# Modulation vectors accumulated on VectorE in two FFNs, convolution taps spread over the last layer, and the convolution's norm placed inside the pooling branch

## Chip, core and metric

The kernel runs on one core of a Trainium2 chip. The metric is device time of one execution in microseconds (us); the kernel before takes 2716.47 us (median of 3 runs).

## The reference, cut to what matters

Two transformer blocks of two layers each run one after the other, on 256 latent tokens and 256 context tokens, 1024 wide. Every layer is steered by six modulation vectors, made from a condition `c` (for the latent tokens) and `c_ctx` (for the context tokens); the last layer of a block needs the context's only for its first two vectors.

```python
# block 1, layer l
m_lat = split(silu(c) @ ada_w[l] + ada_b[l], 6)      # ada_w[l]: 1024 x 6144
m_ctx = split(silu(c_ctx) @ ada_w[l] + ada_b[l], 6)
h = x * (1 + m[1]) + m[0]
x = layer_norm(ALPHA * x + m[2] * mixer(h))
x = layer_norm(ALPHA * x + m[5] * conv_ffn(x * (1 + m[4]) + m[3]))
# block 2, layer l: the same six vectors from w_mod[l], b_mod[l], and
def token_mixer(h, hc, ...):
    u = h @ w_glu; u = u[:, :512] * sigmoid(u[:, 512:])
    u = depthwise_conv(u, conv_w, conv_b)             # 31 taps along the tokens, 512 channels
    y_a = silu(layer_norm(u)) @ w_conv_out
    y_b = differential_attention(h, hc) @ w_attn_out
    y_c = multiscale_pool(h @ w_p) @ w_pool_out
    g = sigmoid(h @ w_g + b_gate)
    return (g0 * y_a + g1 * y_b + g2 * y_c) @ w_out
swiglu(h) = (silu(h @ w1) * (h @ w2)) @ w_ffn_out
```

In the first layer of a block all 512 tokens are carried through, in the second only the 256 latent ones leave the mixer. All data are fp32.

## The kernel before

**Weights and products.** Each weight comes from memory as a 128x1024 tile `wr` (512 KB, `wload`, L143, issued on SP's queue, four buffers). `wsplit` (L149) makes from it a rounded high part `wh` on ScalarE (L154) and the rest `wl` on VectorE or GpSimd (L156), three buffers each. A product is then three matmuls: high by high, high by low, low by high (L163). One weight tile is 24 matmuls.

**Stages in time.** Block 1 layer 0 (mixer, then a 512-token FFN from about 340 us), block 1 layer 1 (mixer, then a 256-token FFN), block 2 layer 0 (mixer from 1110 us, 512-token FFN from about 1720), block 2 layer 1 (mixer from 2120 us, 256-token FFN from 2520). The attentions run under an order written out by `weave`: a list of main entries (one weight tile's products and the evictions that follow), between which the steps of the attention units are put. An entry that does one thing alone is marked `light`. Outside the attentions a scheduler orders the instructions of each engine by its own estimate of time; each engine then executes in that fixed order.

**Modulation vectors.** `ada` (L171) makes a list of work items for the vectors ("parts") of one layer: per part eight slices of 128 rows, then the bias, then a transposition. For a slice the raw tile is loaded and four TensorE matmuls (L195) multiply it by the conditions `cs`, each for 256 of the 1024 columns and each at its own group of 32 columns of the array; the eight slices of a part sum up in one PSUM bank. `run_ada` takes items off the list at fixed places, `stream_ada` puts them into the list of an attention. Block 1 layer 1 has its items begun in the first attention and the remaining 38 in the 512-token FFN that follows. The 58 items of block 2 layer 1 are spread over block 2 layer 0: two with each of its eight heads, the rest in the 512-token FFN.

**512-token FFN** (`ffn`, L1106). Up products come in pairs `j` (a gate tile and a value tile): pairs 0 to 3 for one half of the tokens and then for the other, pairs 4 to 10 for all 512, then the first half of the down products, pairs 11 to 21, and the second half. The products `gH`, `gL` of a pair have 14 buffers. Items of `ada` are taken one after each of the pairs 0 to 3 of the second half, two after each of the pairs 4 to 10, one after each down weight, one after each later pair, and what is left ahead of `mid`.

**Convolution and branches of block 2.** The 31 taps for four groups of 128 channels are 124 VectorE operations (`conv_taps`, L1601; L1605 and L1608), taken one by one from a generator. `tick` in `b2_attn` takes `rate` of them per light entry of the attention; `b2_branches` takes 15 after each of the eight output blocks of the attention's branch ("merged blocks", L1681), and the rest after it. Then `b2_conv_ln` normalises the convolution's result, and the pooling branch (`branch(2, ...)`) and the convolution's branch (`branch(0, ...)`) follow, each with eight merged blocks (L1684).

## Time and profile before

| | before |
|---|---|
| median of 3 runs | 2716.47 us (2715.8 to 2717.38) |
| profiled execution | 2717.76 us, its span 2716.0 us |
| TensorE (PE) busy | 2572.2 us, 95% |
| VectorE (DVE) busy | 1744.9 us, 64% |
| ScalarE (ACT) busy | 1230.1 us, 45% |
| GpSimd (POOL) busy | 405.1 us, 15% |
| mean granted clock of TensorE | 0.981 |
| HBM read | 408.59 MB |

The span runs from the first instruction to the last; the execution's own time holds 1.8 us more around it. Busy shares are averages over stages with different limits, so the windows below are read stage by stage. Matmuls overlap on TensorE: what one costs the queue is seen from the starts of its neighbours, not from its own length.

### The profile page before, as it was taken

Reading aid. Unit: us, or ns where it says so; the run is one execution under the profiler, and the core shown is the slowest. Engines: PE = TensorE matmul, PEld = TensorE weight load, DVE = VectorE, ACT = ScalarE, POOL = GpSimd, SP = SyncE. Lnnn points to the kernel's source line nnn. Section 1 sums busy time; section 2 is a strip of 40 time slices with the busy share of each in tenths; the row PEclk is TensorE's granted clock in tenths of the full one; section 3 lists DMA queues with packets and bytes.
Section 4 is the critical chain, followed back from the end, with each engine's and each line's share of the span. In section 5 each row is a group of like instructions: output and inputs, shape, how many; then the busy total and the mean of one; then the engine's idle time right before and its main releaser. Section 6 shows DMA issues by size and latency. Waiting matters only on the chain. (4 is left out here: it accounts for less than half of the span.)

```text
span 2716.0 us, 41732 instructions
## 1 busy us (share of the span) xinstructions
PE 2572.2 (95%) x16052; PEld 2196.6 (81%) x16052; DVE 1744.9 (64%) x3131; ACT 1230.1 (45%) x2327; POOL 405.1 (15%) x481
## 2 busy tenths in 40 slices
PE   7999899999998899999988999999999999789998
PEld 5787697778876798998976787877777999788997
DVE  5766785355887877577789546632236766986554
ACT  3554453134455555556652324522224566344443
POOL 4221100000121100444320000000000243100000
PEclk9999999999999999999999999999999999899999
DMA  8355765543556665532212234655445421246555
GB/s 274 100 160 173 252 212 174 164 128 118 179 174 230 206 228 182 170 112 90 90 62 78 79 101 156 196 170 162 146 125 161 146 81 65 88 150 197 168 183 148
DMA packets 129831, 412.43 MB, mean 152 GB/s; under 512 B 16640, under 2 KB 24992, under 8 KB 129632
## 3 DMA queue, kind: packets, MB, share of 16 engines
q1 hardware_dynamic: 119296, 386.45, 44.8%
q0 software_dynamic: 10048, 23.30, 2.8%
q8 instruction: 126, 2.06, 0.3%
q14 instruction: 73, 0.60, 0.1%
q10 hardware_dynamic: 288, 0.02, 0.0%
HBM read 408.59 MB, written 1.11 MB: 151 GB/s over the span
## 5 line engine op out<-in xcount | busy, mean ns | idle before, releaser
L154 ACT CAST wh<-wr 128x1024 fp32r<-128x1024 f32 (+2 forms) x580 | 572.3, 990 | 920.3 <-PE mm L163 653.1
L156 DVE TENSOR_TENSOR wl<-wr,wh 128x1024 fp32r<-128x1024 f32 (+2 forms) x494 | 571.3, 1159 | 452.3 <-ACT wh L154 448.9
L163 PE MATMUL mm<-hH,wh 128*128 128x256 f32 (+1 forms) x2176 | 714.1, 329 | 5.1 <-DVE sil L1144 2.3
L163 PE MATMUL mm<-hH,wl 128*128 128x256 f32 (+1 forms) x2176 | 707.9, 326 | 9.1 <-DVE wl L156 9.1
L163 PE MATMUL mm<-hL,wh 128*128 128x256 f32 (+1 forms) x2176 | 707.1, 325 | 0.0
L163 PEld LDWEIGHTS mm<-hH,wh 128*128 128x128 f32 x2176 | 419.0, 193 | 57.4 <-issue 18.3
L163 PEld LDWEIGHTS mm<-hH,wl 128*128 128x128 f32 x2176 | 419.1, 193 | 45.2 <-DVE wl L156 13.0
L163 PEld LDWEIGHTS mm<-hL,wh 128*128 128x128 f32 x2176 | 419.3, 193 | 30.7
L163 PE MATMUL mm<-wh,hH 128*128 128x384 f32 (+1 forms) x864 | 278.5, 322 | 0.7 <-DVE hH L308 0.7
L163 PE MATMUL mm<-wl,hH 128*128 128x384 f32 (+1 forms) x864 | 269.6, 312 | 2.8 <-DVE wl L156 1.8
L163 PE MATMUL mm<-wh,hL 128*128 128x384 f32 (+1 forms) x864 | 269.2, 312 | 0.3 <-DVE hL L312 0.3
L156 POOL TENSOR_TENSOR wl<-wr,wh 128x768 fp32r<-128x768 f32 (+1 forms) x86 | 182.5, 2126 | 260.4 <-ACT wh L154 183.6
L163 PE MATMUL mm<-wl,gH 128*128 128x512 f32 x528 | 205.9, 390 | 2.6 <-DVE wl L156 2.6
L163 PE MATMUL mm<-wh,gH 128*128 128x512 f32 x528 | 208.0, 395 | 0.0
L163 PE MATMUL mm<-wh,gL 128*128 128x512 f32 x528 | 205.9, 390 | 0.0
L163 PEld LDWEIGHTS mm<-wh,hH 128*128 128x128 f32 x864 | 163.9, 190 | 13.9 <-issue 11.0
L163 PEld LDWEIGHTS mm<-wl,hH 128*128 128x128 f32 x864 | 164.0, 190 | 6.2 <-DVE wl L156 2.7
L163 PEld LDWEIGHTS mm<-wh,hL 128*128 128x128 f32 x864 | 163.8, 190 | 0.5 <-DVE hL L312 0.5
L1608 DVE SCALAR_TENSOR_TENSOR cv<-u,cconv_w,cv 128x512 f32<-128x512 f32 (+1 forms) x240 | 162.1, 682 | 2.2
L262 POOL TENSOR_TENSOR rs_r<-rs_v,mhalf 128x1 f32<-128x1 f32 x44 | 40.0, 911 | 630.1 <-DVE rs_v L283 373.9
L163 PEld LDWEIGHTS mm<-wh,gH 128*128 128x128 f32 x528 | 99.1, 188 | 28.4 <-issue 8.6
L163 PEld LDWEIGHTS mm<-wl,gH 128*128 128x128 f32 x528 | 99.2, 188 | 23.3 <-DVE wl L156 3.5
(332 smaller groups left out, 3961.5 us busy)
## 6 DMA issues: line engine op xcount, KB each, us to landing
wr<-in_up SPq DMA_DIRECT2D x192, 512.0 KB, 4.3
wr<-in_dn SPq DMA_DIRECT2D x100, 512.0 KB, 3.7
wr<-in_w_mod SPq DMA_DIRECT2D x96, 512.0 KB, 4.3
wr<-in_ada_w SPq DMA_DIRECT2D x80, 512.0 KB, 4.2
wr<-in_wg SPq DMA_DIRECT2D x48, 512.0 KB, 3.6
wr<-in_glu SPq DMA_DIRECT2D x24, 512.0 KB, 4.2
wr<-in_qkv SPq DMA_DIRECT2D x32, 384.0 KB, 3.2
wr<-in_wo SPq DMA_DIRECT2D x24, 512.0 KB, 4.1
```

The costliest lines, as they stand in the source:

```text
L154: nc.scalar.copy(h[:, :n], w[:, :n])
L156: eng.tensor_tensor(l[:, :n], w[:, :n], h[:, :n], ALU.subtract)
L163: self.nc.tensor.matmul(o, s, m, start=start, stop=stop, skip_group_check=True)
L262: self.nc.gpsimd.tensor_tensor(o, i, self.mhalf[:, 0:n], ALU.pow)
L1608: nc.vector.scalar_tensor_tensor(o, u[:, :, j:j + 256], w[:, c, j:j + 1], o, ALU.mult, ALU.add)
```

## The change

Three things are changed.

1. While a 512-token FFN runs (from pair 4 up to `mid`), a slice of a modulation vector is not multiplied on TensorE. VectorE multiplies the raw tile by the condition's value of each partition and adds it to an accumulator of 128x1024 (`onto`): one accumulator per condition, one buffer each. At a part's last slice TensorE sums the accumulator over the partitions with four matmuls per condition against a vector of ones (`pick`). Parts whose context vector nobody reads (`ctx=2`: all but the first two of the second layers) have one accumulator, the others two. A part that was begun on TensorE goes on in the accumulator and is added to its bank. In block 2 layer 0 no items ride with the attention any more; all 58 go to the FFN, two after each later pair and three after pairs 20 and 21. No item is taken in pairs 0 to 3. `gH` and `gL` have 12 buffers.
2. In block 2's last layer every main entry ticks, not the light ones alone, at a rate of 0.6 instead of 1.5. The taps that are left after the attention are strewn, in both layers, evenly over the eight blocks of the attention's branch and the first five of the pooling branch.
3. The convolution's norm is issued after the fifth block of the pooling branch, not ahead of that branch.

```diff
@@ setup
+        self.pick = cp.tile([P, 33], F32, name="pick")
+        nc.gpsimd.memset(self.pick, 0.0)
+        nc.gpsimd.memset(self.pick[:, 1:2], 1.0)
@@ ada
-    def ada(self, key, blk, w, b, parts=(1, 0, 2, 4, 3, 5)):
+    def ada(self, key, blk, w, b, parts=(1, 0, 2, 4, 3, 5), ctx=6):
+            def quarter(st, j, a, x, start, stop):
+                nc.tensor.matmul(st["pa"][32 * j:32 * j + 32, 0:256], a, x[:, j * 256:(j + 1) * 256], start=start, stop=stop,
+                                 skip_group_check=True, tile_position=(0, 32 * j))
+
+            def onto(wt, st, k, rows):
+                if "acc" not in st:
+                    st["acc"] = [self.acc_pool.tile([P, D], F32, tag=f"acc{r}", name=self.nm("adacc"), bufs=1) for r in range(rows)]
+                    for r in range(rows):
+                        nc.vector.tensor_scalar(st["acc"][r], wt, cs[:, k, r:r + 1], None, ALU.mult)
+                else:
+                    for r in range(rows):
+                        nc.vector.scalar_tensor_tensor(st["acc"][r], wt, cs[:, k, r:r + 1], st["acc"][r], ALU.mult, ALU.add)
-            def prod(wt, m=m, k=0, st=st):
+            def prod(wt, m=m, k=0, st=st, rows=2 if parts.index(m) < ctx else 1):
...
-                for j in range(4):
-                    nc.tensor.matmul(st["pa"][32 * j:32 * j + 32, 0:256], cs[:, k, :], wt[:, j * 256:(j + 1) * 256],
-                                     start=(k == 0), stop=(k == 7), skip_group_check=True, tile_position=(0, 32 * j))
+                if self.acc_pool is not None:
+                    onto(wt, st, k, rows)
+                else:
+                    if "pa" not in st:
+                        st["pa"] = self.psum(self.ada_bank)
+                    for j in range(4):
+                        quarter(st, j, cs[:, k, :], wt, k == 0, k == 7 and "acc" not in st)
+                if k == 7 and "acc" in st:
+                    first = "pa" not in st
+                    if first:
+                        st["pa"] = self.psum(self.ada_bank)
+                    for r, a in enumerate(st["acc"]):
+                        for j in range(4):
+                            quarter(st, j, self.pick[:, 1 - r:33 - r], a, first and r == 0, r == len(st["acc"]) - 1)
@@ ffn
-                    nbuf = 14 if T == 512 else 22
+                    nbuf = 22 if T == 256 else 12
@@
                 for s in range(2):
                     for j in range(self.SKEW):
                         up_pair(j, s, s + 1)
-                        if s:
-                            self.run_ada(ada, 1)
+                self.acc_pool = pool
...
                 for j in range(11, 22):
                     up_pair(j, 0, 2)
-                    self.run_ada(ada, 1)
+                    self.run_ada(ada, 2 if j < 20 else 3)
                 self.run_ada(ada, 100)
+                self.acc_pool = None
@@ b2_attn
-            gr["extra"] = self.stream_ada(ws, ada, 2)
@@
-            if i > n and getattr(main[i], "light", True):
+            if i > n and (not full or getattr(main[i], "light", True)):
                 due[0] += rate
                 while due[0] >= 1:
                     due[0] -= 1
-                    next(taps, None)
+                    next(taps, lambda: None)()
@@ b2_branches
-                for _ in range(15):
-                    next(taps, None)
+                strew()
+
+            left = list(taps)
+            n = -(-len(left) // 13)
+
+            def strew():
+                for f in left[:n]:
+                    f()
+                del left[:n]
             branch(1, "wyb", 8, at, hook)
-            for _ in taps:
-                pass
             pools.close()
@@
-        self.b2_conv_ln(cp, cp, cb["pool"], l, T, nseg, cb["cv"], cc)
-        branch(2, "wyc", 4, mix, lambda oc: None)
+
+        def hook2(oc):
+            strew()
+            if oc == 4:
+                assert not left
+                self.b2_conv_ln(cp, cp, cb["pool"], l, T, nseg, cb["cv"], cc)
+        branch(2, "wyc", 4, mix, hook2)
@@ build
-            a0 += self.ada("b1l1", 1, A["ada_w"][1], A["ada_b"][1])
+            a0 += self.ada("b1l1", 1, A["ada_w"][1], A["ada_b"][1], ctx=2)
...
-            a3 = self.ada("b2l1", 2, A["w_mod"][1], A["b_mod"][1])
+            a3 = self.ada("b2l1", 2, A["w_mod"][1], A["b_mod"][1], ctx=2)
...
-            self.b2_mixer(1, 256, cb[1], lambda: after(1), ws, self.glu_items(ws, 1, cb[1], 0, 1), 1.5)
+            self.b2_mixer(1, 256, cb[1], lambda: after(1), ws, self.glu_items(ws, 1, cb[1], 0, 1), 0.6)
```

The taps' generator now yields functions, called where a tap was taken before. What the order of instructions makes of this is shown at three places; the line numbers are each kernel's own.

VectorE in the first 512-token FFN, one pair's work among the pairs 4 to 10. Before (`acc` are convolutions, `sil` and `gL` the pair's product, `wl` the next weights' low parts):

```order
L156 TENSOR_TENSOR wl_4891<-wr_4888,wh_4890 128x1024
L1121 SCALAR_TENSOR_TENSOR acc_4831<-mm_4772,conv_w_791_3357,acc_4831 128x2x255
L1122 SCALAR_TENSOR_TENSOR acc_4831<-mm_4772,conv_w_791_3357,acc_4831 128x2x255
L1121 SCALAR_TENSOR_TENSOR acc_4835<-mm_4803,conv_w_791_3357,acc_4835 128x2x255
L1122 SCALAR_TENSOR_TENSOR acc_4835<-mm_4803,conv_w_791_3357,acc_4835 128x2x255
L1141 TENSOR_TENSOR sil_4830<-sil_4830,acc_4831 128x512
L1150 TENSOR_TENSOR gL_4842<-sil_4830,gH_4841 128x512
L156 TENSOR_TENSOR wl_4951<-wr_4948,wh_4950 128x1024
L156 TENSOR_TENSOR wl_4982<-wr_4979,wh_4981 128x1024
```

Now (`adacc` is the accumulator):

```order
L1151 SCALAR_TENSOR_TENSOR acc_4622<-mm_4565,conv_w_791_3360,acc_4622 128x2x255
L204 SCALAR_TENSOR_TENSOR adacc_4552<-wr_4806,cs_85,adacc_4552 128x1024
L1152 SCALAR_TENSOR_TENSOR acc_4622<-mm_4565,conv_w_791_3360,acc_4622 128x2x255
L204 SCALAR_TENSOR_TENSOR adacc_4552<-wr_4809,cs_85,adacc_4552 128x1024
L161 TENSOR_TENSOR wl_4730<-wr_4727,wh_4729 128x1024
L1151 SCALAR_TENSOR_TENSOR acc_4626<-mm_4596,conv_w_791_3360,acc_4626 128x2x255
L1152 SCALAR_TENSOR_TENSOR acc_4626<-mm_4596,conv_w_791_3360,acc_4626 128x2x255
L1171 TENSOR_TENSOR sil_4621<-sil_4621,acc_4622 128x512
L161 TENSOR_TENSOR wl_4761<-wr_4758,wh_4760 128x1024
L1180 TENSOR_TENSOR gL_4633<-sil_4621,gH_4632 128x512
```

The slices' two accumulations, which were matmuls on TensorE, stand among the pair's convolutions, ahead of the low parts of the coming weights.

SP's queue at the end of the second 512-token FFN (`in_up` and `in_dn` are FFN weights, `in_w_mod` a modulation slice). Before:

```order
L146 DMA wr_19782<-in_up 128x1024
L146 DMA wr_19813<-in_up 128x1024
L146 DMA wr_19851<-in_w_mod 128x1024
L146 DMA wr_19857<-in_up 128x1024
L146 DMA wr_19888<-in_up 128x1024
L146 DMA wr_19926<-in_w_mod 128x1024
L146 DMA wr_19950<-in_dn 128x1024
L146 DMA wr_19968<-in_dn 128x1024
```

Now:

```order
L151 DMA wr_19663<-in_up 128x1024
L151 DMA wr_19694<-in_up 128x1024
L151 DMA wr_19734<-in_w_mod 128x1024
L151 DMA wr_19743<-in_w_mod 128x1024
L151 DMA wr_19751<-in_w_mod 128x1024
L151 DMA wr_19754<-in_w_mod 128x1024
L151 DMA wr_19757<-in_w_mod 128x1024
L151 DMA wr_19760<-in_w_mod 128x1024
L151 DMA wr_19763<-in_w_mod 128x1024
L151 DMA wr_19766<-in_w_mod 128x1024
L151 DMA wr_19792<-in_dn 128x1024
```

Before, the slices came one by one between the up weights; now eight stand between the last up weight and the first down weight.

VectorE in the attention of block 2's last layer, between two heads' evictions (`cv` is a tap, `f` and `rope` the rotary product of a tile, `v` and `kst` its value and key). Before:

```order
L1371 TENSOR_TENSOR v_21075<-mm_21010,v_21075 128x128
L562 TENSOR_TENSOR kst_21076<-mm_21010,kst_21076 128x2x128
L1371 TENSOR_TENSOR v_21075<-mm_21010,v_21075 128x128
L562 TENSOR_TENSOR kst_21079<-mm_21010,kst_21079 128x2x128
L535 TENSOR_TENSOR f_21158<-qf_20917,rc_20563 128x128
L538 TENSOR_TENSOR rope_4396_21159<-qf_20917,rs_20565 128x4x16 x2
L535 TENSOR_TENSOR f_21158<-mm_21082,rc_20563 128x128
```

Now:

```order
L1401 TENSOR_TENSOR v_20913<-mm_20847,v_20913 128x128
L592 TENSOR_TENSOR kst_20914<-mm_20847,kst_20914 128x2x128
L1401 TENSOR_TENSOR v_20913<-mm_20847,v_20913 128x128
L592 TENSOR_TENSOR kst_20917<-mm_20847,kst_20917 128x2x128
L1638 SCALAR_TENSOR_TENSOR cv_20736<-u_16852,cconv_w_3632_16848,cv_20736 128x256 x2
L565 TENSOR_TENSOR f_20999<-qf_20756,rc_20405 128x128
L568 TENSOR_TENSOR rope_4408_21000<-qf_20756,rs_20407 128x4x16 x2
L565 TENSOR_TENSOR f_20999<-mm_20921,rc_20405 128x128
L568 TENSOR_TENSOR rope_4409_21005<-mm_20921,rs_20407 128x4x16 x2
```

No tap stood here; now taps come between the evictions, one or two at a time. Over the whole layer 42 taps stood ahead of the first merged block of the attention's branch and 82 between its first and last; now these are 62 and 46, and 16 follow in the pooling branch. In layer 0 they were 70 and 54; now 54, 62 and 8.

## Rows read from the trace of the kernel before

**Rows 1.** Windows: start:end, length, busy (x count) of PE, PEld, DVE, ACT, POOL; PEclk, DMA, GB/s.

```profile
340.00:640.00 300.00, 299.75 (x1647) 240.10 (x1647) 175.61 (x248) 117.71 (x161) 12.90 (x22) 1.00 0.53 165
1110.00:1422.00 312.00, 296.72 (x1957) 272.58 (x1956) 225.19 (x493) 176.90 (x470) 120.44 (x97) 0.98 0.31 98
1422.00:1506.00 84.00, 73.37 (x286) 54.84 (x285) 77.45 (x117) 19.81 (x23) 1.61 (x3) 0.94 0.24 76
1506.00:1540.00 34.00, 33.31 (x154) 26.75 (x153) 14.24 (x29) 12.83 (x16) 2.62 (x4) 1.00 0.20 62
1720.00:2050.00 330.00, 326.98 (x1758) 260.33 (x1757) 114.60 (x138) 96.56 (x130) 10.94 (x22) 0.99 0.51 159
2152.00:2303.00 151.00, 146.79 (x1204) 142.77 (x1203) 98.30 (x282) 94.40 (x246) 68.79 (x58) 0.99 0.23 73
2303.00:2343.00 40.00, 34.74 (x245) 32.37 (x245) 35.70 (x83) 21.87 (x52) 10.70 (x18) 0.91 0.24 80
2343.00:2412.00 69.00, 52.28 (x344) 48.74 (x343) 62.72 (x135) 19.07 (x27) 0.33 (x1) 0.78 0.35 108
2412.00:2425.00 13.00, 12.71 (x108) 12.49 (x107) 11.27 (x26) 9.57 (x14) 1.10 (x2) 1.00 0.44 138
2425.00:2490.00 65.00, 62.64 (x497) 61.71 (x497) 45.30 (x74) 29.88 (x43) 1.13 (x2) 0.97 0.65 198
```

**Rows 2.** Windows for the tile `cv`: PE, PEld, DVE (the taps), PEclk, DMA, GB/s.

```profile
1422.00:1506.00 84.00, 0.98 (x6) 0.78 (x6) 40.80 (x55) 0.94 0.24 76
2152.00:2303.00 151.00, 0.00 (x0) 0.00 (x0) 3.40 (x5) 0.99 0.23 73
2303.00:2343.00 40.00, 0.38 (x2) 0.24 (x2) 15.21 (x29) 0.91 0.24 80
2343.00:2412.00 69.00, 1.60 (x6) 0.82 (x6) 37.14 (x82) 0.78 0.35 108
```

**Rows 3.** Windows for line 195, the modulation matmuls: PE, PEld, PEclk, DMA, GB/s.

```profile
340.00:640.00 300.00, 18.77 (x248) 5.39 (x248) 1.00 0.53 165
1110.00:1422.00 312.00, 8.95 (x112) 2.20 (x112) 0.98 0.31 98
1720.00:2050.00 330.00, 20.69 (x272) 5.87 (x272) 0.99 0.51 159
```

**Rows 4.** Timeline of PE, first FFN: start us, us, engine line op tiles xcount.

```profile
422.23 0.39 PE L163 MATMUL mm<-hL,wh 128*128 128x512 f32 x1
422.46 0.39 PE L163 MATMUL mm<-hH,wl 128*128 128x512 f32 x1
422.78 0.64 PE L195 MATMUL ax<-wr,cs 128*32 128x256 f32 x8
...
423.69 0.39 PE L163 MATMUL mm<-hL,wh 128*128 128x512 f32 x1
```

**Rows 5.** Timeline of PE, second FFN, two slices together.

```profile
1802.90 0.39 PE L163 MATMUL mm<-hH,wl 128*128 128x512 f32 x1
1803.22 1.07 PE L195 MATMUL ax<-wr,cs 128*32 128x256 f32 x16
...
1804.56 0.40 PE L163 MATMUL mm<-hL,wh 128*128 128x512 f32 x1
```

**Rows 6.** Instructions on the tile `x`: count, ns min/median/max, first and last start.

```profile
L1065 DVE TENSOR_SCALAR z<-x,bnmv,rs_r x12: 805/812/815, 314.0 to 1109.0; 128x1024 f32<-128x1024 f32 x12
L1278 DVE SCALAR_TENSOR_TENSOR x<-ym,rs_r,x x12: 744/748/753, 1685.3 to 2512.8; 128x512 f32<-128x512 f32 x12
```

**Rows 7.** Groups by form, DVE, 340 to 640 us: busy, mean ns, idle before.

```profile
L156 DVE TENSOR_TENSOR wl<-wr,wh 128x1024 fp32r<-128x1024 f32 x58 | 70.9, 1222 | 79.9 <-ACT wh L154 79.6
```

**Rows 8.** DMA issues: count, size, median us from issue to landing.

```profile
wr<-in_w_mod SPq DMA_DIRECT2D x96, 512.0 KB, 4.3
```

**Rows 9.** Instructions on the tile `cv`, 2152 to 2303 us.

```profile
L1608 DVE SCALAR_TENSOR_TENSOR cv<-u,cconv_w,cv x5: 475/485/1141, 2185.3 to 2302.8; 128x256 f32<-128x256 f32 x5
```

**Rows 10.** Timeline of POOL at 2224 us.

```profile
2224.04 2.40 POOL L156 TENSOR_TENSOR wl<-wr,wh 128x1024 fp32r<-128x1024 f32 x1 [2.18 <-ACT wh L154]
```

More of the change, by code (lines that the diff above doesn't have):

```diff
@@ L1175, in ffn @@
                     up_pair(j, 0, 2)
-                    self.run_ada(ada, 1)
+                    self.run_ada(ada, 2 if j < 20 else 3)
                 self.run_ada(ada, 100)
+                self.acc_pool = None
                 mid()
@@ L1601, in conv_taps, with first, tap @@
         for c in range(4):
-            o = cb["pool"].tile([P, nseg, 286], F32, tag="cu", name=self.nm("cv"), bufs=5)[:, :, 0:256]
-            cb["cv"].append(o)
-            u, w = cb["u"][c], cb["w"]
-            nc.vector.tensor_scalar(o, u[:, :, 0:256], w[:, c, 0:1], cb["b"][:, c:c + 1], ALU.mult, ALU.add)
-            yield
+            def first(c=c):
+                o = cb["pool"].tile([P, nseg, 286], F32, tag="cu", name=self.nm("cv"), bufs=5)[:, :, 0:256]
+                cb["cv"].append(o)
+                nc.vector.tensor_scalar(o, cb["u"][c][:, :, 0:256], cb["w"][:, c, 0:1], cb["b"][:, c:c + 1], ALU.mult, ALU.add)
+            def tap(j, c=c):
+                o = cb["cv"][c]
+                nc.vector.scalar_tensor_tensor(o, cb["u"][c][:, :, j:j + 256], cb["w"][:, c, j:j + 1], o, ALU.mult, ALU.add)
+            yield first
             for j in range(1, 31):
-                nc.vector.scalar_tensor_tensor(o, u[:, :, j:j + 256], w[:, c, j:j + 1], o, ALU.mult, ALU.add)
-                yield
+                yield lambda j=j, tap=tap: tap(j)
     def pool_items(self, ws, l, T, cb):
```

1 line of the change is left out of this document (removed).

## Prediction

> **What bounds the kernel.** The views were read from coarse to fine: the windows by stage, then TensorE's timeline at single instructions, then the costs of VectorE's instructions, then the convolution's taps by window. In both 512-token FFNs TensorE is never idle and VectorE has room [rows 1]: 299.75 of 300 us busy on TensorE against 175.61 on VectorE in the first (340 to 640 us), 326.98 of 330 against 114.60 in the second (1720 to 2050). What leaves TensorE's queue there shortens the stage. In the mixers of block 2 it is the other way round: while the attention branch is merged (1422 to 1506 in layer 0, 2343 to 2412 in layer 1) VectorE is busy 77.45 of 84 and 62.72 of 69 us, and TensorE only 73.37 and 52.28, in layer 1 at a mean granted clock of 0.78, so partly at 1.2 instead of 2.4 GHz. Much of VectorE's time there is taps [rows 2]: 40.80 and 37.14 us. In layer 1's attention before it (2152 to 2303) only 5 taps run.
>
> **1. Modulation products leave TensorE.** The 1024 x 1024 slices are counted in TensorE's records, eight to a slice [rows 3]: 248, 112 and 272 records are 31 slices in the first FFN, 14 in layer 0's attention and 34 in the second FFN, 79 in all. Their price is read from starts. Ordinary 512-column matmuls start 0.23 us apart; with one slice between them, three starts span 423.69 - 422.46 = 1.23 us [rows 4], so a slice costs 1.23 - 2 x 0.23 = 0.77 us. Two slices together: 1804.56 - 1802.90 = 1.66, less 0.46, is 1.20 us [rows 5]. Five such pairs occur in each FFN. So TensorE gets rid of 21 x 0.77 + 5 x 1.20 = 22.2 us, 14 x 0.77 = 10.8 us and 24 x 0.77 + 5 x 1.20 = 24.5 us. Added: a summing set against `pick` at each part's end, like one slice: 4 in the first FFN (3.1 us), 8 in the second (6.2 us). Net: -19.1, -10.8, -18.3, together **-48.2 us**. From below the price is bounded by columns alone: two passes of 256 columns at the pace of [rows 4] are 0.23 us. I take 0.77, because it is the spacing itself.
>
> The Trainium skill ("TensorE: Matmul & The Clock Gate", Part 3: Packing small matmuls) says that column tiles on different 32-column groups run at once, at about 4 ns each, which speaks against this change: the removed work would be nearly free. By that a slice would take about 0.24 us and this sum be 16 instead of 48; the spacing in this trace disagrees.
>
> VectorE gets 95 operations on 128x1024. Twelve are first ones, priced as the two-scalar operation at 0.81 us [rows 6]; 83 accumulate. For those the nearest row is the two-input subtraction of the same size, 1.22 us [rows 7]; a form with a scalar pointer takes 0.748 on 512 elements [rows 6], so 1.50 is the upper end. I take 1.22. First FFN: 27 x 1.22 + 4 x 0.81 = 36 us, VectorE 212 of the 281 us left (75%). Second: 56 x 1.22 + 8 x 0.81 = 75 us, 189 of 312 (61%). So this lies under the matmuls, but not without friction. An accumulation at the head of VectorE's queue waits for its slice to land; behind it stand convolutions and the low halves `wl` that TensorE needs next. The accumulator has one buffer, so a part's first operation waits until TensorE has reached the summing set of the part before; the set in turn waits for the last accumulation. Twelve such meetings, each between nothing and an operation or so (1.5 us): 0 to 20, I take **+8 us**. With 14 buffers cut to 12, pair 12 reuses buffer 0, last read before pair 11's matmuls on the same engine: nothing, and were that cover gone, one tile's wait. No slices ride with the first four pairs: SP's queue gets shorter there. Each part's four bias transfers move along on GpSimd's queue, which is busy 10.94 of 330 us in the second FFN: nothing. Two memsets at the start lie under the first weights' landing: nothing.
>
> **2. The end of the second FFN.** 14 slices move here from the attention, and SP's queue now has eight of them in a row between the last up weights and the first down weights. Four raw buffers serve all. The first of the eight is accumulated only after the previous part's sum, two tiles (24 matmuls x 0.23 = 5.4 us each) before TensorE runs dry; the fifth can be loaded only when the first is done, 4.3 us to landing [rows 8]; four more accumulations end about 2 us after TensorE has finished. Then come the summing set (0.8), and the first down weight, queued behind on SP and on VectorE (1.2). About 4 us idle, and some of the time after it at the lower clock: **+6 us**, bounds 0 and 15 (every one of the last four loads paid in full).
>
> **3. Layer 0's mixer.** By the order 54 taps stand ahead of the first merged block where 70 did, and 39 between the first and the sixth where 54 did. Those 15 fewer take 15 x 0.742 = 11 us off VectorE's 77.45 in [rows 1], about 66, below TensorE's 73.37: most of its 10.6 us of idle time goes. Later blocks get 31 taps, 23 us, where VectorE is busy 14.24 of 34 us (from 1506) [rows 1]: just under TensorE's pace, a few us lost. Net -8, and -2 for lighter attention: **-10**, bounds 0 and -20. The norm starts later, but its chain stood under matmuls (12.71 of 13 us busy from 2412 in layer 1) and still has three blocks and a branch behind it: nothing; if that cover failed, its transposes would stall TensorE for the last tap, which the upper end holds.
>
> **4. Layer 1's mixer.** By the order 46 taps lie between first and last merged block of the attention branch, where 82 did. VectorE's need falls by 36 x 37.14/82 = 16 to 46 us. TensorE's 52.28 busy us at clock 0.78 are 41 at full clock, so VectorE stays the longer; at its present fill (62.72/69) the stretch takes 51 instead of 69: -18. Before it (2303 to 2343) 29 taps become about 10, against 5.3 us of idle TensorE: -5. Sixteen taps in the pooling branch, 7 us where VectorE is at 45.30 of 65: +2. The attention takes some 40 more taps. At 0.45 to 0.68 us (5 in 3.40) VectorE goes from 98.30 to 116 to 126 of 151 us; nearest is layer 0's attention, VectorE 225.19 of 312 with TensorE idle 4.9% against 2.8% here: **+5**, bounds 0 and 26. Net **-16**, bounds +10 and -26.
>
> **Sum.** -48.2 + 8 + 6 - 10 - 16 = -60. The profiled execution took 2717.76 us (span 2716.0), 1.3 above the median of the three runs; I forecast **2657 us**.
>
> **Rivals.** *A. Taps choke layer 1's attention.* One tap there took 1141 ns where the median is 485 [rows 9], beside a weight subtraction of 2.40 us on GpSimd [rows 10], which is busy 68.79 of 151 us. If each of 40 added taps takes 1.14 - 0.48 longer and the softmax chain waits for it, the attention loses 26 instead of 5: 2678. For it: GpSimd is busy for 46% of the stretch; against: only one tap of five was hit. The Trainium skill ("SBUF — State Buffer", Who interferes with whom) states the cause: a two-input VectorE operation and a GpSimd operation that reads SBUF exclude each other for a whole instruction. The row agrees.
>
> *B. The slices were nearly hidden.* At 0.23 us each, 67 net slices save 16 instead of 48: 2689. Against it stands the spacing of starts in [rows 4].
>
> *C. Slower: loads block VectorE.* TensorE used to absorb the wait for a slice; now VectorE does, with `wl` behind it. If each of 65 slices in the FFNs held it for a whole landing of 4.3 us, its need would be 212 + 133 = 345 against 281, and 189 + 146 = 335 against 312: 64 + 23 more, less the 8 already counted: 2736. It decides from about 2.2 us of wait per slice in the first FFN. Against it: loads are asked for four buffers ahead, and DMA is at 0.53 there. A mild form ends within 0.2%.
>
> *D. Everything fits.* No friction, no tail, both mixers at their better bounds: 2657 - 14 - 10 - 10 = 2623.
>
> **How the numbers follow.** Forecast 0.62, A 0.14, B 0.06, C 0.07, D 0.11. The range 2630 to 2692 holds the forecast with its bounds on friction and tail, A and B; C and D are left out. A measurement can tell about 0.2%, 5 us, from no change. Only C is not faster: 0.05 slower and 0.02 the same, 0.93 faster.
>
> **What would show it.** In the FFNs: TensorE without gaps, the stages some 15 and 8 us shorter (the second after its gap), VectorE at about 75 and 60%. At the second FFN's end a gap of a few us before the first down product, put down to the accumulator or to `wl`. In layer 1: taps even through the attention, merged blocks closer to 6 us apart, granted clock near 1. The forecast is wrong if TensorE waits for `wl` or the accumulator all through the FFNs (C), if the FFN stages hardly shrink with no new gap (B), or if layer 1's attention grows by over 10 us (A).

## The result and the profile after

The changed kernel takes 2655.65 us (median of 4 runs, 2653.86 to 2658.98) against 2716.14 us (median of 4 runs of the kernel before beside them): ratio 0.978, 95% interval 0.9763 to 0.9797. The forecast was 2657 us, faster. The profiled execution took 2655.9 us, its span 2654.1, 61.9 us less than the one that the prediction was worked out on.

Busy time by engine, from the page of the kernel after:

```profile
PE 2515.9 (95%) x15516; PEld 2183.4 (82%) x15516; DVE 1852.0 (70%) x3226; ACT 1230.0 (46%) x2329; POOL 407.9 (15%) x483
```

TensorE is busy 56 us less than before and VectorE 107 us more; the other engines hardly changed.

To say where the time went, the span of each kernel is cut at the same events: a stage of an FFN begins or ends with its first `sil` or the end of its down products, a branch with its first and its eighth merged block, an attention with the first block after it. Lengths in us, each from one profiled execution; "part 1 alone" and "2 and 3 alone" are the first two experiments below:

| stage | before | after | part 1 alone | 2 and 3 alone |
|---|---|---|---|---|
| first 512-token FFN | 377.0 | 360.9 | 360.0 | 377.1 |
| layer 0: attention | 275.8 | 270.6 | 271.2 | 276.2 |
| layer 0: attention branch | 99.1 | 86.7 | 101.4 | 86.6 |
| layer 0: pooling and convolution branches | 137.7 | 137.6 | 137.4 | 138.0 |
| second 512-token FFN | 393.9 | 380.4 | 382.2 | 393.6 |
| layer 1: attention | 200.8 | 206.0 | 201.3 | 206.7 |
| layer 1: attention branch | 68.6 | 48.4 | 66.3 | 48.3 |
| layer 1: pooling and convolution branches | 76.4 | 76.0 | 76.9 | 75.7 |

From before to after these stages give -62.7 us together. Stages in which nothing was changed differ by up to 3 us from one profile to the next (layer 1's attention took 203.8 to 206.7 us in the seven profiles with its 62 taps and low halves as in the kernel after), so a difference of 1 or 2 us in one row says nothing. What TensorE waits in a stage, its length less TensorE's busy time, is steadier: 14.1 to 14.6 us in the same seven.

The windows of the kernel after that answer to [rows 1] (same columns; in order the first FFN, layer 0's attention, the second FFN, layer 1's attention, its attention branch, its other two branches; the last row is layer 0's attention branch):

```profile
340.00:640.00 300.00, 296.57 (x1500) 249.80 (x1499) 216.67 (x290) 121.41 (x168) 12.37 (x22) 1.00 0.54 170
1136.00:1407.00 271.00, 253.19 (x1560) 236.10 (x1560) 194.99 (x451) 156.43 (x438) 94.05 (x78) 0.99 0.21 63
1687.00:1990.00 303.00, 299.33 (x1510) 251.39 (x1509) 175.06 (x194) 93.28 (x126) 13.71 (x24) 0.99 0.58 184
2096.00:2302.00 206.00, 191.68 (x1532) 185.43 (x1531) 160.83 (x398) 119.69 (x302) 83.23 (x77) 0.98 0.25 79
2302.00:2350.00 48.00, 43.81 (x345) 41.76 (x345) 47.28 (x98) 18.50 (x26) 0.25 (x1) 1.00 0.50 155
2350.00:2426.00 76.00, 73.45 (x597) 71.67 (x596) 60.63 (x114) 40.87 (x57) 3.16 (x4) 1.00 0.61 187
...
1407.00:1494.00 87.00, 83.77 (x355) 67.17 (x354) 83.48 (x119) 22.36 (x27) 1.15 (x3) 0.98 0.29 88
```

VectorE is at 72% in the first FFN and 58% in the second (75 and 61 were forecast). In layer 1's attention branch TensorE needs 43.81 us at clock 1.00 for what took 52.28 at 0.78 [rows 1], and VectorE fills 47.28 of 48 us: it is the bound there, as before, with less to do. For part of the 69 us before, TensorE had waited for VectorE in a special way. The transposes of the convolution's norm (L1774) stood in TensorE's order inside this branch, each behind the last tap of its channels (view of TensorE's waits, 2343 to 2412 us: us in total, times, longest):

```profile
PE ax L1774 <- DVE cv L1608: 7.9, 2, 4.2
```

That is 7.9 of the 16.7 us in which TensorE was idle there. The kernel after has no such wait in its branch.

The new operations, instructions on the tile `adacc` in the first FFN (columns as in [rows 6]):

```profile
L204 DVE SCALAR_TENSOR_TENSOR adacc<-wr,cs,adacc x27: 1273/1284/1286, 389.7 to 568.3; 128x1024 f32<-128x1024 f32 x27
...
L201 DVE TENSOR_SCALAR adacc<-wr,cs x4: 744/745/746, 384.7 to 538.1; 128x1024 f32<-128x1024 f32 x4
```

An accumulation takes 1.284 us where 1.22 were taken from [rows 7], a first one 0.745 where 0.81 were taken from [rows 6]. The longest waits of VectorE for a slice's load, from the view of waits (engine, tile and line <- releaser: us in total, times, longest), first FFN and most of the second:

```profile
DVE adacc L204 <- DMA wr<-in_ada_w: 29.9, 17, 5.9
```

```profile
DVE adacc L204 <- DMA wr<-in_w_mod: 45.7, 24, 4.7
```

That is about 1.0 us for each slice in both (31 slices; 48, most of them in that window): the loads do hold VectorE, but well below the 2.2 us from which rival C would have decided. Rival C's sum counted 65 slices, as on TensorE before; the changed kernel accumulates 79, 48 of them in the second FFN, so at a whole landing each it would have come out still later than 2736 us.

### The profile page after: what moved, and what is told of

It reads as the page before. It is cut to its first block, busy times and chain, and to the rows that moved or that the text cites. A ratio compares the mean times of both kernels' runs of the same rounds, so it can differ in the third digit from the quotient of the medians.

```text
span 2654.1 us, 40807 instructions
## 1 busy us (share of the span) xinstructions
PE 2515.9 (95%) x15516; PEld 2183.4 (82%) x15516; DVE 1852.0 (70%) x3226; ACT 1230.0 (46%) x2329; POOL 407.9 (15%) x483
## 4 chain that ended last, share of the span: by engine, by line
PE 70%; DVE 13%; issue 6%; DMA 6%; ACT 4%; POOL 2%; SPq 0%; POOLq 0%; DVEq 0%; ACTq 0%
PE mm L168 62%; PE ax L168 3%; DVE wl L161 2%; DMA wr<-in_ada_w 2%; PE mm L194 1%; PE ax L600 1%; POOL rs_r L292 1%; DMA wr<-in_w_mod 1%; PE ax L611 1%; DVE ptl L615 1%; DMA gbc<-gd 1%; DMA s0w<-in_ada_w 1%; DVE cv L1638 1%; DVE p L1516 1%; ACT wh L159 1%
## 5 line engine op out<-in xcount | busy, mean ns | idle before, releaser
L168 PE MATMUL mm<-wh,gL 128*128 128x512 f32 x528 | 206.0, 390 | 0.0
L1638 DVE SCALAR_TENSOR_TENSOR cv<-u,cconv_w,cv 128x512 f32<-128x512 f32 (+1 forms) x240 | 168.4, 704 | 2.6
L204 DVE SCALAR_TENSOR_TENSOR adacc<-wr,cs,adacc 128x1024 f32<-128x1024 f32 x83 | 105.6, 1283 | 78.3 <-DMA wr<-in_w_mod 48.1
```

The source lines that it names most:

```text
L168: self.nc.tensor.matmul(o, s, m, start=start, stop=stop, skip_group_check=True)
L204: nc.vector.scalar_tensor_tensor(st["acc"][r], wt, cs[:, k, r:r + 1], st["acc"][r], ALU.mult, ALU.add)
L1638: nc.vector.scalar_tensor_tensor(o, cb["u"][c][:, :, j:j + 256], cb["w"][:, c, j:j + 1], o, ALU.mult, ALU.add)
```

## The experiments

Each run has its own runs of the kernel before beside it (median 2715.3 to 2716.8 us). The intervals of the ratios reach 4 to 7 us to either side. Those of runs 5, 6, 8, 9, 10 and 12 overlap the changed kernel's, so what these runs show rests on the lengths of their stages and on TensorE's waits, and not on the totals alone. Diffs show the lines that matter; `...` stands for lines that are not shown.

**1. Part 1 alone.** The changed kernel with the old taps and the old place of the norm.

```diff
-            if i > n and (not full or getattr(main[i], "light", True)):
+            if i > n and getattr(main[i], "light", True):
...
-                strew()
...
+                for _ in range(15):
+                    next(taps, lambda: None)()
             branch(1, "wyb", 8, at, hook)
+            for f in taps:
+                f()
...
-        branch(2, "wyc", 4, mix, hook2)
+        self.b2_conv_ln(cp, cp, cb["pool"], l, T, nseg, cb["cv"], cc)
+        branch(2, "wyc", 4, mix, lambda oc: None)
...
-            self.b2_mixer(1, 256, cb[1], lambda: after(1), ws, self.glu_items(ws, 1, cb[1], 0, 1), 0.6)
+            self.b2_mixer(1, 256, cb[1], lambda: after(1), ws, self.glu_items(ws, 1, cb[1], 0, 1), 1.5)
```

> The changed kernel with its first part alone: slices accumulated on VectorE in the 512-token FFNs and taken out of layer 0's attention; taps and norm as before. Theory (the parts add up, and slices cost TensorE 0.77 us each): the first FFN is 16 us shorter, the second 13, the attention 5 to 11, while 16 taps fewer in layer 0's attention push up to 12 us into its VectorE-bound branch: 2680 to 2692 us. Rival B (slices were nearly hidden at 0.23 us): 2700 or more. Rival (the two parts need each other): near 2716.

Measured: 2681.22 us, ratio 0.9873 (0.9858 to 0.9888). Its stages are in the table: the FFNs and layer 0's attention are shorter, by 17.0, 11.7 and 4.6 us; layer 1's attention branch, in which nothing was changed, differs by 2.3. The 16 taps that moved into layer 0's attention branch (70 where 54 were) cost 2.3 us there, not up to 12. Twelve of that branch's taps now stand behind its sixth block, where before none did.

**2. Parts 2 and 3 alone.** The kernel before with the new taps and norm; `acc_pool` stays empty, 14 buffers, slices at their old places.

```diff
-                    nbuf = 22 if T == 256 else 12
+                    nbuf = 22 if T == 256 else 14
...
-                self.acc_pool = pool
+                        if s:
+                            self.run_ada(ada, 1)
...
-                    self.run_ada(ada, 2 if j < 20 else 3)
+                    self.run_ada(ada, 1)
...
+            gr["extra"] = self.stream_ada(ws, ada, 2)
```

> The changed kernel with its second and third part alone: taps strewn and the norm inside the pooling branch, modulation vectors as before on TensorE. Theory: layer 1's branch is 20 us shorter and its attention 5 longer, layer 0's branch 8 to 12 shorter: 2686 to 2694 us. Rival A (taps choke layer 1's attention): 2705 or more.

Measured: 2687.28 us, ratio 0.9888 (0.9871 to 0.9904). The two halves give -34.7 and -28.7 us, together -63.4 against -60.5 for the whole change: they add, within what medians scatter.

**3. What a slice costs on TensorE.** The kernel before with the matmuls of the middle slices (k = 1 to 6) of each part left out in both FFNs, 49 slices; their loads stay, and their part of the modulation vectors is missing.

```diff
-                for j in range(4):
+                for j in range(0 if self.skip and 0 < k < 7 else 4):
...
+                self.skip = True
...
+                self.skip = False
```

> The kernel before, with the matmuls of 49 of the 65 slices in the two 512-token FFNs left out (slices 1 to 6 of each part; their loads stay), so it computes other modulation vectors. It prices a slice on TensorE by itself. Theory (0.77 us, 0.60 in pairs): 30 to 37 us less, 2679 to 2686. Rival B (0.23 us): 11 less, 2705.

Measured: 2678.30 us, ratio 0.9856 (0.9842 to 0.9871): -37.6 us, just beyond the expected 30 to 37 and 0.77 us for each slice. It is the spacing of starts in [rows 4], and rival B's 0.23 falls.

**4. What the accumulations cost.** The changed kernel with those of k = 1 to 6 left out of the sums.

```diff
-                else:
+                elif k == 7:
                     for r in range(rows):
```

> The changed kernel with VectorE's accumulations of slices 1 to 6 left out (loads, first operations, last accumulations and summing sets stay), so it computes other modulation vectors. Theory (VectorE has room; friction and tail were put at 8 and 6 us): 3 to 12 us less, 2644 to 2653. Rival C in a mild form (VectorE's accumulations hold TensorE up in the FFNs): 20 or more less. If nothing was lost to friction: within 3 us of 2655.7.

Measured: 2647.48 us, ratio 0.9746 (0.9731 to 0.9761), 8.2 us below the changed kernel. By stages 2.5 us are in the first FFN (358.4) and 3.8 in the second (376.6). So what these accumulations bring of friction and tail is 6 to 8 us, where the sum had 14; the first and last operation of each part stay in this run. In the second FFN the time comes off at the end (the stretch from the first down products to the second 2.3 us shorter, the second down products 1.9), as it does in run 5; friction outside the tail is seen in the first FFN at most, 2.5 us.

**5. The tail spread.** The changed kernel with three slices after each of the pairs 11 to 20, so that none is left to queue in a row ahead of the down weights.

```diff
-                    self.run_ada(ada, 2 if j < 20 else 3)
+                    self.run_ada(ada, 3 if j < 21 else 2)
```

> The changed kernel with the last eight summed slices of the second 512-token FFN spread over the pairs before it, three a pair instead of two, so that none is queued in a row ahead of the down weights. If the row of eight costs what the stage marks of the earlier runs suggest (2.5 us at the end of the second up product, 1.8 us in the down product): 2650 to 2654 us. If there is no such stall, or three slices in a pair bring as much friction as the tail did: 2655 to 2660 us.

Measured: 2651.81 us, ratio 0.9758 (0.9743 to 0.9772), 3.8 us less; the second FFN's second set of up products, with the gap behind it, loses 2.3 us and the down products behind it 1.6. The timelines of TensorE at this place (columns as in [rows 4], with the idle time before and its releaser in brackets), in the kernel after:

```profile
1997.02 0.38 PE L239 MATMUL ax<-idn,adas 128*128 128x128 f32 x2
1999.42 0.64 PE L194 MATMUL ax<-adacc,pick 128*32 128x256 f32 x8 [2.02 <-DVE adacc L204]
2000.27 1.22 PE L168 MATMUL mm<-wh,gH 128*128 128x512 f32 x2 [0.20 <-ACT wh L159]
2001.73 0.79 PE L168 MATMUL mm<-wl,gH 128*128 128x512 f32 x1 [0.25 <-DVE wl L161]
```

and with the tail spread:

```profile
1997.43 0.39 PE L168 MATMUL mm<-hH,wl 128*128 128x512 f32 x1
1997.75 0.64 PE L194 MATMUL ax<-adacc,pick 128*32 128x256 f32 x8
1998.32 0.50 PE L168 MATMUL mm<-wh,gH 128*128 128x512 f32 x1
1998.65 0.39 PE L168 MATMUL mm<-wl,gH 128*128 128x512 f32 x1
```

The gap of 2.02 us before the summing set is the forecast wait for the last accumulation. The matmuls behind it are drawn out (1.22 us for two, then 0.79, where one takes 0.39 elsewhere), which the spread tail hardly shows. VectorE's timeline there names what the summing set waited for, the last loads of the row:

```profile
1994.00 1.28 DVE L204 SCALAR_TENSOR_TENSOR adacc<-wr,cs,adacc 128x1024 f32<-128x1024 f32 x1 [0.95 <-DMA wr<-in_w_mod]
1995.65 1.29 DVE L204 SCALAR_TENSOR_TENSOR adacc<-wr,cs,adacc 128x1024 f32<-128x1024 f32 x1 [0.37 <-DMA wr<-in_w_mod]
1997.99 1.28 DVE L204 SCALAR_TENSOR_TENSOR adacc<-wr,cs,adacc 128x1024 f32<-128x1024 f32 x1 [1.05 <-DMA wr<-in_w_mod]
```

**6. Layer 0's slices back in its attention, on TensorE.**

```diff
+            gr["extra"] = self.stream_ada(ws, ada, 2)
```

> The changed kernel with layer 0's slices, two for each head, back in its attention and on TensorE, so that the second FFN keeps 34 slices and has no row of eight at its end. If those slices filled stretches in which TensorE waited for the softmax anyway: layer 0's attention 5 us longer (270.6 to about 276), the second FFN 4 to 9 us shorter, 2650 to 2657 us in all. If a slice costs its full 0.77 us there, as in the FFNs: attention 10.8 us longer, 2657 to 2663 us.

Measured: 2650.96 us, ratio 0.9758 (0.9744 to 0.9773). The attention grows by 5.8 us to 276.4, not by 10.8, and the second FFN shrinks by 7.1 to 373.3. That is 0.41 us for each of 14 slices, about half of their 0.77. But the slices' entries tick too, so 16 taps come back with them (70 stand ahead of the attention branch, where the kernel after has 54); no run parts the two. The attention's windows, before, after and with the slices back, show what became of the slices' time:

```profile
1151.00:1427.00 276.00, 262.85 (x1671) 237.94 (x1670) 212.08 (x471) 157.16 (x438) 98.61 (x86) 0.99 0.28 89
1136.00:1407.00 271.00, 253.19 (x1560) 236.10 (x1560) 194.99 (x451) 156.43 (x438) 94.05 (x78) 0.99 0.21 63
1138.00:1414.00 276.00, 263.01 (x1667) 238.15 (x1666) 211.95 (x471) 157.00 (x438) 98.30 (x85) 0.98 0.28 89
```

With the slices back TensorE is busy 9.8 us more, near the 10.8 that 14 slices were priced at, and idle 4.8 us less (13.0 for 17.8); against the kernel before the change took 9.7 us of work away and left 4.7 more of waiting. The waits of TensorE (same view as above), first in the kernel after:

```profile
PE ax L600 <- DVE ptl L615: 8.3, 6, 1.9
PE ax L1564 <- DVE os L1559: 4.3, 8, 1.5
PE ax L600 <- ACT p L1503: 1.9, 5, 0.4
```

and with the slices back:

```profile
PE ax L600 <- ACT p L1504: 4.5, 7, 2.3
...
PE ax L600 <- DVE ptl L615: 1.7, 1, 1.7
PE ax L1565 <- DVE os L1560: 1.3, 1, 1.3
```

In these rows TensorE waits 14.5 us without slices, for the probabilities (`p`), their low parts (`ptl`) and the heads' outputs (`os`), and 7.5 with them; the rows not shown hold 3.3 and 5.2 us. So about half of the slices' time had filled waits.

**7. The norm ahead of the pooling branch, the taps left after the attention over eight blocks.**

```diff
-            n = -(-len(left) // 13)
+            n = -(-len(left) // 8)
...
-        branch(2, "wyc", 4, mix, hook2)
+        self.b2_conv_ln(cp, cp, cb["pool"], l, T, nseg, cb["cv"], cc)
+        branch(2, "wyc", 4, mix, lambda oc: None)
```

> The changed kernel with the convolution's norm ahead of the pooling branch again and the taps that are left spread evenly over the eight blocks of the attention branch, as before the change; part 1 and the strewn taps stay. If the shorter attention branch comes from taps that now stand behind it: layer 0's branch 3 to 6 us longer (86.7 to about 91), layer 1's 3 to 7 us longer (48.4 to about 54), pooling branches the same to 2 us shorter, 2660 to 2668 us. If moving the norm does nothing by itself and all of the gain in layer 1 comes from the strewn taps: within 3 us of 2655.7.

Measured: 2669.18 us, ratio 0.982 (0.9801 to 0.9839), 13.5 us above the changed kernel, a little over the expected range. Layer 0's attention branch takes 93.7 us (+7.0) with 70 taps for 62, layer 1's 56.1 (+7.7) with 53 for 46, and layer 1's pooling branch is 2.8 longer. In layer 0 eight taps of 0.74 us would be 6 of the 7 us, though 54 taps or 62 made no difference there (86.6 and 86.7 us, run 2 and the kernel after). Against run 1, with 70 taps in layer 0's branch and the norm ahead in both, the even spread alone makes that branch 7.7 us shorter (101.4 to 93.7). In layer 1 seven taps are 3.4 us of VectorE, and the stretch lost twice that. Its window:

```profile
2305.00:2361.00 56.00, 48.68 (x347) 46.33 (x345) 51.03 (x106) 18.81 (x26) 0.28 (x1) 0.91 0.43 132
```

TensorE is idle for 7.3 of 56 us, and the mean granted clock is 0.91 where it was 1.00, so part of the stretch ran at 1.2 instead of 2.4 GHz. All its waits are for VectorE, for weights' low parts and for `pH`, the high part of the pooling's result (2305 to 2361 us):

```profile
PE mm L168 <- DVE wl L161: 4.1, 4, 1.0
PE mm L168 <- DVE pH L338: 3.1, 4, 1.3
```

None is a transpose of the norm waiting for a tap: with even taps this wait of the kernel before (7.9 us) is gone although the norm stands ahead again.

**8. Half the rate of taps in layer 1's attention.** 32 taps ahead of the branch, 57 in it, 35 behind it.

```diff
-            self.b2_mixer(1, 256, cb[1], lambda: after(1), ws, self.glu_items(ws, 1, cb[1], 0, 1), 0.6)
+            self.b2_mixer(1, 256, cb[1], lambda: after(1), ws, self.glu_items(ws, 1, cb[1], 0, 1), 0.3)
```

> The changed kernel with half the rate of taps in the last layer's attention (0.3 instead of 0.6): 32 taps stand before the attention branch, 57 inside it, 35 behind it. If a tap costs only VectorE's time wherever it stands, and the attention branch and the pooling branch wait for VectorE while the attention only partly does: attention 3 to 4 us shorter (206 to about 203), attention branch 48 to 53 us, pooling branch 5 to 8 us longer, 2660 to 2666 us in all. If taps are dearer in the attention than in the branches (rival A in a milder form): below 2655 us.

Measured: 2649.02 us, ratio 0.9748 (0.9729 to 0.9766); the profiled execution took 2653.54, the longest of the four. The attention is 196.0 us, 10 shorter rather than 3 to 4; the branch 54.7 and the others 78.1. The taps' sum in the attention went from 45.4 us for 62 to 19.1 for 32, and TensorE's waits there from 14.3 us to 7.7:

```profile
2095.00:2291.00 196.00, 188.33 (x1527) 182.22 (x1527) 135.51 (x368) 119.30 (x301) 82.68 (x76) 0.99 0.27 83
```

By stages 30 taps fewer saved 0.33 us each in the attention, 11 more cost 0.57 each in the attention branch, and 19 more 0.11 each behind it. So the first reading fell, a tap in the attention costs three times what it put; but the second is right only against the pooling branch, for the dearest place is the attention branch. In this one profile the three stages give -1.6 us together, and the medians -6.6.

**9. The low halves of layer 1's attention on VectorE.** This takes GpSimd's 24 subtractions out of the stretch and leaves the taps as they are in the changed kernel.

```diff
-            ws = Stream(self, 12)
+            ws = Stream(self, 1000)
```

> The changed kernel with the low halves of the last layer's attention weights on VectorE instead of GpSimd: 24 more subtractions of 1.22 us on VectorE, none on GpSimd. If the long taps (eleven of 62 between 0.6 and 2.7 us) are VectorE held up by GpSimd's subtractions: no tap in the attention over 0.5 us, the taps' sum there 45 to about 30 us, the other stretched instructions 16 us shorter together, which pays for the 29 us that are added; the attention 200 to 208 us, 2650 to 2660 us in all. If something else stretches them (a load, the queue): taps stay long, VectorE has 29 us more, the attention 215 us or more and 2664 us or more in all.

Measured: 2649.06 us, ratio 0.9752 (0.9738 to 0.9767), a microsecond below the expected range; the attention 200.8 us. The taps in the attention of the kernel after (instructions on the tile `cv`), and then of this one:

```profile
L1638 DVE SCALAR_TENSOR_TENSOR cv<-u,cconv_w,cv x60: 469/478/2656, 2100.7 to 2295.4; 128x256 f32<-128x256 f32 x60
```

```profile
L1638 DVE SCALAR_TENSOR_TENSOR cv<-u,cconv_w,cv x60: 473/478/502, 2099.4 to 2287.6; 128x256 f32<-128x256 f32 x60
```

The longest tap fell from 2656 to 502 ns at the same median (the other two taps of 62 are first operations of a channel group, of another form). The window of this attention:

```profile
2095.00:2296.00 201.00, 189.37 (x1529) 183.84 (x1528) 158.86 (x425) 119.90 (x303) 24.48 (x53) 0.98 0.26 79
```

VectorE is as busy as in the kernel after (158.86 against 160.83 us) although it does 24 subtractions more: the work took the place of being held up. And the stage is back at the 200.8 us that it had before the change. Of the 5.2 us 2.7 are waits of TensorE (14.3 to 11.6); the rest is busy time, which varies as much between equal programs. Two waits in the kernel after show how hold-ups reach TensorE. The first of them, VectorE, GpSimd, then TensorE:

```profile
2171.16 3.02 DVE L1638 SCALAR_TENSOR_TENSOR cv<-u,cconv_w,cv 128x256 f32<-128x256 f32 x2
2174.29 2.12 DVE L1513 SCALAR_TENSOR_TENSOR cs<-s0s,nlam,r1s 128x1 f32<-128x1 f32 x1
2177.11 0.68 DVE L615 TENSOR_TENSOR ptl<-ax,pth 128x512 fp32r<-128x512 f32 x1
```

```profile
2171.48 4.91 POOL L161 TENSOR_TENSOR wl<-wr,wh 128x1024 fp32r<-128x1024 f32 x2 [0.89 <-ACT wh L159]
```

```profile
2177.85 0.79 PE L168 MATMUL ax<-sT,sT 128*128 128x512 f32 x1 [3.16 <-DVE ptl L615]
```

Two subtractions in a row hold up a tap and then the small `cs` (median 220 ns), a factor of the probabilities; `ptl`, behind them in VectorE's order, comes late, and TensorE waits 3.16 us. The same stands at 2219 to 2225 us. Both waits, 6.3 us together, are gone in this run and shrink to 0.5 us in run 8. The subtractions that left GpSimd had kept TensorE waiting directly too, for 1.6 us, so not all of what this run gains is VectorE's.

**10. Two accumulators everywhere.** Context vectors that nobody reads are summed too.

```diff
-            a0 += self.ada("b1l1", 1, A["ada_w"][1], A["ada_b"][1], ctx=2)
+            a0 += self.ada("b1l1", 1, A["ada_w"][1], A["ada_b"][1])
-            a3 = self.ada("b2l1", 2, A["w_mod"][1], A["b_mod"][1], ctx=2)
+            a3 = self.ada("b2l1", 2, A["w_mod"][1], A["b_mod"][1])
```

> The changed kernel with two accumulators for every part, the unread context vectors too (the result of these is not used): 63 more VectorE operations on 128x1024, 81 us, and eight more summing sets on TensorE. If VectorE has room in both FFNs: eight sets of 0.77 us, 6 us, and as much friction as the first 83 accumulations had (8 us) or less, 2660 to 2670 us. If VectorE is near its limit (rival C's point): the low halves come late all through the FFNs and most of the 81 us shows, over 2690 us.

Measured: 2660.13 us, ratio 0.9792 (0.9776 to 0.9809), 4.5 us above the changed kernel. The windows of both FFNs:

```profile
340.00:640.00 300.00, 299.75 (x1555) 253.08 (x1554) 250.31 (x324) 123.83 (x170) 13.07 (x22) 1.00 0.55 172
1687.00:1990.00 303.00, 298.83 (x1522) 250.40 (x1521) 199.77 (x217) 92.56 (x125) 13.39 (x24) 0.99 0.57 182
```

VectorE is at 83% in the first, and TensorE has no gap there; the stage is 1.9 us shorter than in the kernel after, within what equal stages differ. The second FFN is 7.4 us longer, 5.6 of them behind its last up products, where TensorE waits in one piece for a down weight whose load stands behind the row of eight:

```profile
2004.59 1.22 PE L168 MATMUL mm<-wh,gH 128*128 128x512 f32 x2 [6.26 <-ACT wh L159]
```

So VectorE still had room up to that tail, and rival C stays far; what the 32 operations more cost in the second FFN is paid mostly there.

**11. A mixture.** Tail spread (5), half rate (8), and of the taps left in layer 1 five to each block of the attention branch and eleven to each of the pooling branch's first five.

```diff
...
-            n = -(-len(left) // 13)
+            n = [5] * 8 + [-(-(len(left) - 40) // 5)] * 5 if T == 256 else [-(-len(left) // 13)] * 13
...
```

> The changed kernel with three edits: the slices at the second FFN's end spread (three a pair), half the rate of taps in the last layer's attention, and of the taps left there five to each block of the attention branch and the rest, eleven a block, in the pooling branch's first five. 32 taps then stand ahead of the attention branch, 47 inside it, 45 behind it. If the earlier runs' parts add (tail -3.9 us, half rate -6.6 us) and ten taps fewer in the attention branch save 0.5 us each while ten more in the pooling branch cost between 0.1 and 0.5 us: 2640 to 2648 us. If the pooling branch is full by now: taps cost their whole 0.48 us and the norm is late, 2648 us or more.

Measured: 2646.03 us, ratio 0.9739 (0.9725 to 0.9754), an interval that lies wholly below the changed kernel's 0.9763 to 0.9797. Attention 197.0, branch 48.1, the others 81.4 us: ten taps moved from the attention branch to the pooling branch saved 6.6 us and cost 3.3.

**12. The mixture with (9).**

> The kernel of the run before with 32 taps in the last layer's attention, the spread tail and the filled pooling branch, and the attention's low halves on VectorE as well. If half the rate and the move of the low halves gain by the same thing, that GpSimd holds VectorE up less, there is little left to gain twice: the 32 taps lose 4 us of stretching and other instructions 16, while VectorE gets 29 us: attention 195 to 201 us, 2643 to 2650 us in all. If they gain by two different things (fewer instructions ahead of the softmax chain, and no hold-ups): 6 us more off, attention about 191, 2638 to 2642 us.

Measured: 2645.88 us, ratio 0.9743 (0.9717 to 0.9768); the attention 195.6 us. Nothing more was gained, as the first reading has it. By stages the two overlap in part: 30 taps fewer are worth 9 to 10 us beside GpSimd (206.0 to 196.0 and 197.0) and 5.2 without it (200.8 to 195.6); the low halves' move is worth 5.2 with 62 taps and 1.4 with 32. TensorE's waits in the stage say the same more plainly: 14.3 to 11.6 us with 62 taps, 8.0 to 8.7 with 32.

## Why the prediction was right, and which terms were not

The direction, the bound and the total came out: -60.5 us measured between medians, -60 forecast. But the total is nearer than its terms, whose errors went both ways.

**Slices off TensorE.** The price of 0.77 us is shown by run 3, against rival B and against the rule of the Trainium skill ("TensorE: Matmul & The Clock Gate", Part 3) that the prediction weighed. The first FFN lost 16.1 us where 15 were forecast, the second 13.5 where 8 were. What failed in the second is the size of two terms: friction was put at 8 us for both FFNs and the tail at 6; run 4 puts both together at 6 to 8, and run 5 the tail at 3.8, so that friction is left at 2 to 4. The tail has the form that was foretold (a gap at the accumulator, then the first down weights late, then drawn-out matmuls); of "about 4 us idle" the timeline shows 2.5.

**Layer 0's attention** was the largest miss: -12.8 us forecast (10.8 for slices, 2 for lighter taps), -5.2 measured. The step that failed is to take the slices' work off the stage's length in full, as in an FFN without waits. The work itself was priced well: TensorE is busy 9.7 us less. But 4.7 us of it became waiting for VectorE and ScalarE; [rows 1] showed TensorE idle for 15 of 312 us in this stage before, and a slice that stands where TensorE would wait is not worth its length. Run 6 shows it from the other side. That 16 taps fewer in the stage save 2 us is shown by no run, since taps and slices went together in all of them.

**Layer 0's attention branch**: -8 forecast, -12.4 measured, and with 2 and 3 alone -12.5 with 54 taps inside it, the number that stood there before. So fewer taps are not needed for it. Runs 1 and 7 put the even spread by itself, at 70 taps, at 7.7 us; what parts run 7's 93.7 us from 86.7, the norm's place or eight taps fewer, no run separates. As the step had argued, the spread does most of it, but it was priced too low. "A few us lost" in the later blocks did not show: the last two of the attention branch took 22.7 us against 22.2, the branches after it 137.6 against 137.7.

**Layer 1.** The attention branch lost 20.2 us where 18 were forecast, with VectorE at 98% of it and TensorE at full clock. The prediction got there by VectorE's need and did not see that 7.9 us of TensorE's idle time were the norm's transposes behind late taps. The pooling branch lost nothing (+2 forecast). The attention was to stay about equal, +5 for 40 more taps and -5 for its crowded end; it grew by 5.2, and TensorE's waits in it by 4.8 (9.5 to 14.3). Here rival A was right in its mechanism and wrong in its price. The taps were held up by 45.4 - 62 x 0.478 = 15.8 us, against 25.0 - 42 x 0.478 = 4.9 before. Two of TensorE's waits, 6.3 us together, follow from hold-ups (run 9's rows). Run 9 takes all hold-ups away but gives VectorE 29 us of subtractions, and the stage loses 5.2 us, 2.7 of them waits. So on the path they cost some 3 to 6 us, not 26.

**The norm's place** shows no cost in the branches behind it, as forecast, and it is what allows taps behind the attention branch: run 7, without it, gives 13.5 us back, where parts 2 and 3 are worth 28.7. That run changes the spread with it; the norm's move by itself was not tried.

**Open.** Why run 8's attention got shorter than that of the kernel before (196.0 against 200.8 us, with 32 taps for 42) isn't settled. The taps' hold-ups are much the same in both (4.9 and 19.1 - 32 x 0.478 = 3.8 us). TensorE waits 1.8 us less (7.7 for 9.5) and is busy some 3 us less, which equal programs differ by too, at a granted clock of 0.99 for 0.97:

```profile
2142.00:2343.00 201.00, 191.53 (x1531) 185.11 (x1530) 143.30 (x378) 118.91 (x301) 81.88 (x77) 0.97 0.25 80
```

The low clock of before stands where 29 taps were crowded into the last 40 us, 0.91 there [rows 1]; that the even spread in their place is the reason is argued, and no run shows it alone.

## What to carry to other kernels

Price work that leaves a busy engine by the spacing of its neighbours' starts, and do so in the very stage it leaves: the same slice was worth 0.77 us where TensorE never waited and about half of that where it had waits to fill. Work that is hung into a stage as filler should be spread so that no block gets more than the engine has free there, and kept away from the moments when GpSimd reads SBUF beside a two-input VectorE instruction. When transfers are moved to another place in a queue, look at what stands at the end: eight in a row cost 3.8 us here, as much as all the other friction of the change or more.

## What the runs showed of the hardware

VectorE's hold-ups were sharper than the one tap of [rows 9] let expect. In the kernel after, 11 of the 62 taps in layer 1's attention take over 0.6 us, and each of these overlaps a GpSimd subtraction `wl` and ends 0.28 us after it. One of them, VectorE and then GpSimd:

```profile
2151.98 2.05 DVE L1638 SCALAR_TENSOR_TENSOR cv<-u,cconv_w,cv 128x256 f32<-128x256 f32 x1
2153.95 1.27 DVE L1471 TENSOR_REDUCE pnm<-ax 128x1 f32<-128x512 f32 x2
```

```profile
2151.35 2.40 POOL L161 TENSOR_TENSOR wl<-wr,wh 128x1024 fp32r<-128x1024 f32 x1 [0.36 <-ACT wh L159]
```

The subtraction ends at 2153.75 and the tap at 2154.03. Other VectorE instructions with two inputs on SBUF are held up too (`rope` up to 2428 ns at a median of 218, `qst` 2489 at 284, the one-element `cs` 2119 at 220), while the reductions `pnm` from PSUM, 8 of 32 of which overlap a subtraction, never take over 692 ns at a median of 678. The Trainium skill ("SBUF — State Buffer", Who interferes with whom) says that a VectorE instruction with two SBUF inputs and a GpSimd instruction that reads SBUF exclude each other, for the whole instruction. These rows agree, and run 9, where the subtractions left GpSimd, agrees as well.
